# Making the chunk matrices of a delta-rule branch ahead of its value convolutions in a hybrid encoder layer

## The chip, the cores and the metric

The kernel runs on one core of a Trainium2 chip. The metric is the device time of one execution in microseconds (us). The engines are named as in the profile: PE (TensorE, matrix products), DVE (VectorE), ACT (ScalarE), POOL (GpSimd) and SP (SyncE, whose queue issues the transfers). The times of before are a median of three runs and one profiled execution.

## The reference

One layer on 1024 tokens of width 1024, in float32. `h` is the normalised input; one combined projection of `h` feeds three mixers and their gates.

```python
h = rms_norm(x, mix_norm_w)
dn_qkv, dn_z, dn_b, dn_a, a_q, a_k, a_v, x_q, gate_logits = split(h @ w_in)
# A: bidirectional gated delta rule, 4 heads of 128, chunks of 64 tokens
dq, dk, dv = split(silu(centred_depthwise_conv(dn_qkv, w)))      # 5 taps
dq, dk = l2_normalize(dq), l2_normalize(dk)
lmat = where(strict, (kb @ kc.T) * decay, 0)      # 64 x 64 for each chunk, head and direction
sol = triangular_solve(lmat, [vb, kb * exp(gc)])  # unit lower triangular
attn_intra = (qc @ kc.T) * decay                  # then a scan over the 16 chunks, both ways
# B: attention, 8 query and 2 key heads of 64: rms_norm of q and k, axial rotation, softmax
# C: cross attention, 4 heads of 128, into 256 memory tokens
merged = sum(gates * (branches @ w_branch)); x = x + merged @ w_out
x = x + square(relu(rms_norm(x) @ w_up)) @ w_down
out = rms_norm(x, final_norm_w)
```

## The kernel before

Every product is made of three: each operand is split into a high and a low part (`split`: ACT casts the high part, DVE or POOL subtracts for the low part), and `gemm` sums high·high, low·high and high·low in PSUM. Weights arrive as `w_raw` (512 KB) by `wunit` or `wtok`.

The order of each engine's instructions is fixed when the kernel is built: a scheduler follows the dependencies and its own estimate of times, and within an engine instructions run in that order, one after the other. All transfers are issued on SP's queue.

The stages before the scan, with the names that the prediction uses:

- **Start** (L229 to L285). Eight tiles `xt` of 128 tokens are loaded, squared and summed on ACT (`jk`), scaled by their norm factor and by the norm weight `wbc` on DVE (L278), and transposed by PE into `hTh` and `hTl`.
- **Convolutions.** `conv_tile(ct)` projects 128 channels with 48 matmuls of 512 columns, and forms five taps on DVE: L404 multiplies the first, L409 adds the four others; L417 and L418 finish. Tiles 0 to 7 are queries and keys, 8 to 11 the values; the latter go to `vn_d` in memory.
- **Preparation.** `prep(m)`, once for each of eight pairs of chunks: products of keys and queries (`kq`) and a sum of log decays (`rb`, made by POOL) on PE, `df` and `dd` on DVE (L482 to L493), an exponential on ACT, a factor `nbeta` on POOL. The result goes to `at_d` and `xs_d` in memory.
- **Inverse.** `X`, 128 partitions of 64 x 64, is loaded from `xs_d`; each partition holds one matrix. For j from 1 to 62, L705 makes an outer product into `tm` and L706 adds it to `X`; L708 scales `X` by `bcol`, and it goes to `ts_d`. All of it runs on DVE.
- **Beside the inverse** stand generators that are advanced in turn: `keys()` and `queries()` (24 calls of `rope_norm`, whose results `khl` and `qhl` PE transposes), and `gate_z()` (`z_th`), `mem_norm()`, `memory()` (`mTl`, `mhi`, `mlo`) and `queries_x()` (`xh`, `xl`). `rope_norm` copies the projection to `r_x` (ACT), multiplies it by two rows of the rope table (POOL, L560 and L561), squares and sums each head (ACT, L563), adds the parts (DVE, L568 and L569) and multiplies by the factor of each head (DVE, L570).
- **Gates.** `gates()` makes the matmuls of the three gates; `fill(n)` takes some of them where PE would have none. Then follow the scan (which reads `ts_d`), the two attentions, the branch products, the output projection and the feed-forward part. At the end each of eight tiles `o` is scaled by its norm factor and stored (`finish`, L1148).

Of the kernel before, what the change touches and what calls it, by code (L numbers as in the profile page):

```python
# [9 lines left out]
F32 = mybir.dt.float32  # L10
F32R = mybir.dt.float32r
# [75 lines left out]
def hybrid_block(tc, x, mem, mix_norm_w, w_in, dn_conv_w, dn_a_log, dn_dt_bias, dn_norm_w, q_norm_w, k_norm_w,  # L87
# [147 lines left out]
    wdn = cor.tile([P, 1], F32, name="wdn")  # L235
    ld(out=wdn, in_=dn_norm_w.rearrange("o d -> d o"))
    dve.tensor_scalar(out=wdn, in0=wdn, scalar1=0.5, scalar2=None, op0=ALU.mult)

    tst = ExitStack()
    tkp = pool(tst, "tkp", bufs=2)  # L240

    def wtok(c0):
        hi = tkp.tile([P, 8, 256], F32R, name="t_hi", tag="t_hi", bufs=1)
        lo = tkp.tile([P, 8, 256], F32R, name="t_lo", tag="t_lo", bufs=1)
        for k in range(0, 8, 4):
            raw = wst.tile([P, 4, 256], F32, name="w_raw", tag="w_raw")
            ld(out=raw, in_=w_in[k * P:(k + 4) * P, c0:c0 + 256].rearrange("(k p) c -> p k c", p=P))
            split(hi[:, k:k + 4], lo[:, k:k + 4], raw, wlo[0])
        return hi, lo

# [3 lines left out]
    p0 = pool(st, "p0", bufs=2, side="right")  # L254
    first = {}
    wbc = p0.tile([P, D], F32, name="wbc", bufs=1)
    for m in range(8):
        if m == 0:
            xts = []
            for i in range(8):  # L260
                xt = p0.tile([P, D], F32, name="xt", tag="xt", bufs=8)
                ld_rows(xt, x, i)
                xts.append(xt)
                if i == 0:
                    ld(out=wbc, in_=mix_norm_w.broadcast_to([P, D]))
                if i == 1:
                    braw = wst.tile([P, 8, 64], F32, name="w_raw", tag="w_raw")
                    bhl = tkp.tile([P, 8, 128], F32R, name="b_hl", tag="t_hi", bufs=1)
                    ld(out=braw, in_=w_in[:, C_BA:C_BA + 64].rearrange("(k p) c -> p k c", p=P))
                    split(bhl[:, :, 0:64], bhl[:, :, 64:128], braw)  # L270
                if i == 3:
                    wlo[0] = gp
                    for ct in (4, 0):
                        first[ct] = wunit(w_in[:, ct * P:(ct + 1) * P], 8, P)
                    wlo[0] = None
# [117 lines left out]
    def conv_tile(ct):  # L393
# [70 lines left out]
    def prep(m):  # L464
# [87 lines left out]
    def rope_norm(hi, lo, src, nh, tab, m, sc, bi):  # L552
# [139 lines left out]

    sst = ExitStack()
    sv = pool(sst, "sv", side="right")
    X = sv.tile([P, 64, 64], F32, name="X")
    tm = sv.tile([P, 1024], F32, name="tm")
    bcol = sv.tile([P, 64], F32, name="bcol")
    ld(out=X, in_=xs_d.rearrange("m f a r c -> (m f a) r c"))
    for m in range(8):
        for f in range(2):  # L700
            ld(out=bcol[m * 16 + f * 8:m * 16 + f * 8 + 8], in_=bt_d[:, m, :, f])
    for j in range(1, 63):
# [439 lines left out]
    def factor(m, j):  # L1142
# [96 lines left out]
```

## Time and profile before

| | us |
|---|---|
| median of 3 runs | 1975.61 (1975.19 to 1977.64) |
| the profiled execution | 1976.33 |
| its span, first to last instruction | 1974.5 |
| PE busy | 1900.6 (96%) |
| DVE busy | 1169.2 (59%) |
| ACT busy | 731.8 (37%) |
| POOL busy | 397.2 (20%) |

The difference between span and time of the execution, 1.8 us, is what lies around the first and the last instruction. The granted TensorE clock is 0.988 of full speed in the mean. Busy time is an average over stages; the rows further below take single stages out of it.

### The profile page before, as it was taken

To read this page: it belongs to the slowest core of one execution; us is meant where nothing else is said; L and a number is where in the kernel's file an instruction comes from. 1 tells how busy PE (TensorE), PEld (TensorE's weight loads), DVE (VectorE), ACT (ScalarE), POOL (GpSimd) and SP (SyncE) were. 2 spreads that over 40 slices of the span, in tenths; PEclk is the share of its full clock that TensorE was granted. 3 is DMA by queue.
4 is the path that set the end of the run, shared out by engine and by line. 5 is a ranking of instruction groups with operands and counts; after the bars stand their busy time and mean duration, and the time that the engine had idled before them with its cause. 6 is when DMAs were issued, how large, how long until landed. Compare 5 with 4: busy or idle time off the path is not lost.

```text
span 1974.5 us, 26282 instructions
## 1 busy us (share of the span) xinstructions
PE 1900.6 (96%) x10229; PEld 1611.6 (82%) x10229; DVE 1169.2 (59%) x1701; ACT 731.8 (37%) x1453; POOL 397.2 (20%) x309
## 2 busy tenths in 40 slices
PE   6999897799999999999999999999999999999997
PEld 5888787688998888888888878888888888888885
DVE  4778879993576666666635463444443444444445
ACT  4344343332555666666642131321121212112124
POOL 3003657851251000000000520100010101001013
PEclk9999998899999999999999999999999999999998
DMA  8235743447654222222146455231111102121113
GB/s 170 76 107 149 226 139 110 118 127 243 191 163 133 85 94 75 86 75 86 59 150 201 157 180 161 74 120 40 55 54 33 54 33 65 43 64 46 41 43 86
DMA packets 232893, 207.82 MB, mean 105 GB/s; under 512 B 44800, under 2 KB 196544, under 8 KB 232256
## 3 DMA queue, kind: packets, MB, share of 16 engines
q1 hardware_dynamic: 232768, 206.13, 34.7%
q8 instruction: 81, 1.33, 0.3%
q14 instruction: 44, 0.36, 0.1%
HBM read 148.91 MB, written 57.18 MB: 104 GB/s over the span
## 4 chain that ended last, share of the span: by engine, by line
PE 74%; DVE 6%; POOL 3%; DMA 2%; issue 2%; ACT 1%; SPq 0%; POOLq 0%; DVEq 0%; ACTq 0%
PE ps L81 40%; PE ps_mm L81 20%; PE ps_t L84 3%; PE ps_sm L81 3%; PE ps_t L81 3%; PE ps_s L81 3%; PE ps_sp L81 2%; DVE tm L705 2%; DVE X L706 1%; POOL r_t L560 1%; DMA w_raw<-in_w_out_dram 1%; POOL r_t L561 1%; POOL r_rs L138 0%; DMA X<-xs_d 0%; DVE o L1152 0%
## 5 line engine op out<-in xcount | busy, mean ns | idle before, releaser
L81 PE MATMUL ps_mm<-hTh,w_hi 128*128 128x512 f32 x704 | 286.1, 406 | 3.5 <-ACT hTh L141 3.4
L81 PE MATMUL ps_mm<-hTl,w_hi 128*128 128x512 f32 x704 | 283.9, 404 | 0.0
L81 PE MATMUL ps_mm<-hTh,w_lo 128*128 128x512 f32 x704 | 277.7, 395 | 2.4 <-POOL w_lo L142 2.4
L1140 DVE TENSOR_TENSOR o<-o,ps 128x512 f32<-128x512 f32 (+1 forms) x257 | 171.3, 683 | 97.0 <-PE ps L81 95.5
L81 PE MATMUL ps<-hfh,w_hi 128*128 128x512 f32 x512 | 199.6, 391 | 0.0
L81 PE MATMUL ps<-wdh,al 128*128 128x512 f32 (+1 forms) x514 | 199.6, 389 | 0.0
L81 PE MATMUL ps<-wdl,ah 128*128 128x512 f32 (+1 forms) x514 | 199.6, 389 | 0.0
L81 PE MATMUL ps<-hfl,w_hi 128*128 128x512 f32 x512 | 199.6, 390 | 0.0
L81 PE MATMUL ps<-hfh,w_lo 128*128 128x512 f32 x512 | 199.5, 390 | 0.0
L142 POOL TENSOR_TENSOR wdl<-w_raw,wdh 128x1024 fp32r<-128x1024 f32 x32 | 76.4, 2397 | 601.1 <-ACT wdh L141 601.1
L81 PE MATMUL ps<-wdh,ah 128*128 128x512 f32 (+1 forms) x514 | 188.7, 389 | 0.0
L1132 ACT ACTIVATE f_r<-ps 128x512 f32<-128x512 f32 x64 | 38.1, 595 | 363.7 <-PE ps L81 363.7
L142 DVE TENSOR_TENSOR w_lo<-w_raw,w_hi 128x1024 fp32r<-128x1024 f32 x78 | 100.0, 1282 | 121.0 <-ACT w_hi L141 120.6
L141 ACT CAST w_hi<-w_raw 128x1024 fp32r<-128x1024 f32 x96 | 100.9, 1051 | 171.6 <-PE ps_mm L81 104.0
L1133 DVE TENSOR_TENSOR f_r<-f_r 128x512 f32<-128x512 f32 x64 | 55.3, 865 | 183.3 <-ACT f_r L1132 183.3
L81 PEld LDWEIGHTS ps_mm<-hTh,w_lo 128*128 128x128 f32 x704 | 133.7, 190 | 28.0 <-POOL w_lo L142 2.6
L81 PEld LDWEIGHTS ps_mm<-hTh,w_hi 128*128 128x128 f32 x704 | 133.7, 190 | 27.9 <-ACT hTh L141 3.8
L81 PEld LDWEIGHTS ps_mm<-hTl,w_hi 128*128 128x128 f32 x704 | 133.9, 190 | 20.2
L1072 POOL TENSOR_TENSOR g_acc<-g_acc,g_l 128x512 f32<-128x512 f32 x28 | 41.4, 1481 | 509.8 <-ACT g_yh L141 475.4
L142 DVE TENSOR_TENSOR ptl<-ps_t,pth 128x512 fp32r<-128x512 f32 x128 | 86.6, 687 | 60.0 <-ACT pth L141 59.7
L81 PEld LDWEIGHTS ps<-wdh,al 128*128 128x128 f32 x514 | 96.6, 188 | 19.9
L81 PEld LDWEIGHTS ps<-wdh,ah 128*128 128x128 f32 x514 | 96.5, 188 | 19.8
(288 smaller groups left out, 4045.9 us busy)
## 6 DMA issues: line engine op xcount, KB each, us to landing
w_raw<-in_w_in_dram SPq DMA_DIRECT2D x50, 512.0 KB, 4.1
w_raw<-in_w_up_dram SPq DMA_DIRECT2D x32, 512.0 KB, 4.1
w_raw<-in_w_down_dram SPq DMA_DIRECT2D x32, 512.0 KB, 3.6
g_d<-gt SPq DMA_DIRECT2D x48, 256.0 KB, 2.0
g_l<-g_d SPq DMA_DIRECT2D x24, 512.0 KB, 3.4
w_raw<-in_w_branch_dram SPq DMA_DIRECT2D x12, 512.0 KB, 4.1
y_raw<-y_d SPq DMA_DIRECT2D x12, 512.0 KB, 3.6
xt<-in_x_dram SPq DMA_DIRECT2D x16, 256.0 KB, 9.9
```

Of the source, the lines that this page charges most:

```text
L81: return self._put(self.tc.nc.tensor.matmul(*a, **k))
L84: return self._put(self.tc.nc.tensor.transpose(*a, **k))
L141: act.copy(out=hi, in_=src)
L142: (eng or dve).tensor_tensor(out=lo, in0=src, in1=hi.bitcast(F32), op=ALU.subtract)
L560: gp.tensor_tensor(out=t1, in0=x0, in1=bc(tab[:, 0, m], 1, nh), op=ALU.mult)
L561: gp.tensor_tensor(out=t2, in0=x0, in1=bc(tab[:, 1, m], 1, nh), op=ALU.mult)
L705: dve.tensor_tensor(out=t, in0=bc(X[:, j + 1:, j], 2, j), in1=bc(X[:, j, 0:j], 1, n), op=ALU.mult)
L706: dve.tensor_tensor(out=X[:, j + 1:, 0:j], in0=X[:, j + 1:, 0:j], in1=t, op=ALU.add)
L1072: (dve if bi == 2 and mt > 5 else gp).tensor_tensor(out=acc[mt][:, c], in0=acc[mt][:, c], in1=t, op=ALU.add)
L1132: act.activation(out=r, in_=ps, func=AF.Relu)
L1133: dve.tensor_tensor(out=r, in0=r, in1=r, op=ALU.mult)
L1140: dve.tensor_tensor(out=o[m][:, c], in0=o[m][:, c], in1=ps, op=ALU.add)
```

## The change

Five pieces:

1. Start: all `xt` tiles are allocated first; the norm weight comes as one row of 4 KB, which PE multiplies by a column of ones into 128 partitions (two matmuls, two copies on ACT), where 512 KB were loaded before. Transfers are issued in another order. The first halves of two convolution projections are made straight behind the transposes (`head`).
2. The first tap of a convolution is an ACT instruction (12 in all).
3. `prep` for all eight pairs, and the load of `X` and `bcol`, stand ahead of the value convolutions. `X`, `tm` and `bcol` therefore have memory of their own from early on, and the pool `tkp` (rope table, weights of keys and queries) is opened only when the pools of the convolutions are closed.
4. L570 becomes one ACT instruction for each head (four for a query unit, two for a key unit).
5. The end: the last two tiles are finished behind the loop, tile 7 first; the first half of each is stored by ACT's queue, the second by SP's.

```diff
+    sst = ExitStack()
+    sv = pool(sst, "sv")
...
+    ld_rows(xts[0], x, 0)
+    ld(out=wrow, in_=mix_norm_w)
+    ld(out=ca, in_=ca_d)
...
+        pe.matmul(ps, lhsT=one1, rhs=wrow[:, c:c + 512], start=True, stop=True)
+        act.copy(out=wbc[:, c:c + 512], in_=ps)
...
-                    ld(out=wbc, in_=mix_norm_w.broadcast_to([P, D]))
...
+    head = {}
+    for ct in (4, 0):
+        head[ct] = ps_mm()
+        proj_ch(head[ct], *first[ct], 0)
...
-        dve.tensor_scalar(out=acc, in0=xn, scalar1=cw[:, ct, 2:3], scalar2=None, op0=ALU.mult)
+        act.activation(out=acc, in_=xn, func=AF.Copy, scale=cw[:, ct, 2:3])
...
+    for m in range(8):
+        prep(m)
+
+    X = sv.tile([P, 64, 64], F32, name="X")
...
+    ld(out=X, in_=xs_d.rearrange("m f a r c -> (m f a) r c"))
...
     for h in range(4):
         vt = to_token(conv_tile(8 + h))
         ld(out=dram_tiles(vn_d, h), in_=tiles(vt))
-    for m in range(8):
-        prep(m)
 
     cst.close()
     prs.close()
     gst.close()
+    tst = ExitStack()
+    tkp = pool(tst, "tkp", bufs=2, side="right")
...
-        dve.tensor_tensor(out=x0, in0=x0, in1=bc(rs, 2, 64), op=ALU.mult)
+        for h in range(nh):
+            act.activation(out=x0[:, h], in_=x0[:, h], func=AF.Copy, scale=rs[:, h:h + 1])
...
+    def store(q, m, c):
+        for h, j in enumerate((m, 15 - m)):
+            q.dma_start(out=out[j * 64:(j + 1) * 64, c], in_=o[m][h * 64:(h + 1) * 64, c])
...
+        if m > 5:
+            store(act, m, slice(0, 512))
...
+            store(nc.sync, m, slice(512, 1024))
```

Three places show how the order of the instructions moves. PE at the first preparation, before: `ps_mm` is a convolution's projection (here the last of them), `kq` the first product of a preparation, `rb` the sum of decays; `ps_mm_2087` is a projection of the z gate.

```order
L81 MATMUL ps_mm_1611<-hTh1_150,w_lo_1577 128x512
L81 MATMUL ps_mm_1611<-hTh1_150,w_hi_1576 128x512
L81 MATMUL ps_mm_1611<-hTl1_152,w_hi_1576 128x512
L81 MATMUL ps_mm_1611<-hTh1_150,w_lo_1577 128x512
L81 MATMUL ps_dn_1663<-kq_1660 64x64 x9
L84 MATMUL ps_t_1562<-ca_73,c_x_1496 128x128 x4
L84 MATMUL ps_t_1568<-ca_73,c_x_1496 128x128 x4
L81 MATMUL ps_dn_1663<-kq_1660 64x64 x7
L81 MATMUL ps_dn_1680<-rb_1681,onb_394 128x512
L81 MATMUL ps_dn_1680<-rb_1684,onb_394 128x512
L81 MATMUL ps_dn_1703<-kq_1700 64x64 x16
L81 MATMUL ps_mm_2087<-hTh0_149,w_hi_2082 128x512
```

The same place on PE with the change; `ps_mm_1848` is the third value convolution.

```order
L81 MATMUL ps_mm_1848<-hTh0_147,w_hi_1840 128x512
L81 MATMUL ps_mm_1848<-hTl0_149,w_hi_1840 128x512
L81 MATMUL ps_mm_1848<-hTh0_147,w_lo_1841 128x512
L81 MATMUL ps_mm_1848<-hTh0_147,w_hi_1840 128x512
L84 MATMUL ps_t_1741<-ca_73,c_x_1675 128x128 x2
L81 MATMUL ps_dn_1332<-kq_1329 64x64 x16
L81 MATMUL ps_dn_1349<-rb_1350,onb_453 128x512
L81 MATMUL ps_dn_1349<-rb_1353,onb_453 128x512
L81 MATMUL ps_dn_1372<-kq_1369 64x64 x16
L84 MATMUL ps_t_1741<-ca_73,c_x_1675 128x128 x2
L84 MATMUL ps_t_1747<-ca_73,c_x_1675 128x128 x4
L81 MATMUL ps_mm_1848<-hTl0_149,w_hi_1840 128x512
```

Before, all 576 convolution matmuls stand ahead of the first `kq`; now 493 do, and 84 follow between the preparations.

SP around the load of `X`, before: `at_d` and `xs_d` are results of preparations, `ka_d`, `kb_d` and `vz_d` those of key units, `bcol` a factor of the inverse.

```order
L97 DMA vz_d_124<-vt_2150 128x128
L97 DMA at_d7_117<-dd_1968 128x512
L97 DMA vz_d_124<-vt_2235 128x128
L97 DMA vz_d_124<-vt_2326 128x128
L97 DMA xs_d_118<-dd_1968 64x8x64 x2
L97 DMA ka_d_122<-kab_2121 256x1x128
L97 DMA kb_d_123<-kab_2121 256x1x128
L97 DMA vz_d_124<-vt_2411 128x128
L97 DMA X_4243<-xs_d_118 128x4096
```

With the change: `mt` are the memory tokens, `mwb` their norm weight, `w_raw` the first two weights of the z gate.

```order
L97 DMA at_d7_115<-dd_1637 128x512
L97 DMA xs_d_116<-dd_1637 64x8x64 x2
L97 DMA X_1649<-xs_d_116 128x4096
L97 DMA vn_d_106<-c_tok_1995 128x8x128
L97 DMA mwb_2020<-in_mem_norm_w_dram 128x1024
L97 DMA mt_2022<-in_mem_dram 128x1024
L97 DMA mt_2035<-in_mem_dram 128x1024
L97 DMA rope_2048<-in_rope_dram 128x1024
L97 DMA qkw_2051<-in_q_norm_w_dram 128x64
L97 DMA qkw_2051<-in_k_norm_w_dram 128x64
L97 DMA w_raw_2114<-in_w_in_dram 128x8x128
L97 DMA w_raw_2292<-in_w_in_dram 128x8x128
```

The loads of memory tokens, rope table and z weights, which stood far ahead of the `X` load, now stand behind it.

DVE at the end of the inverse, before: L708 is the last instruction on `X`; `xl` is the low part of a cross-attention query, `w_lo` that of a weight of the gates, `u` (L787) belongs to the scan.

```order
L705 TENSOR_TENSOR tm_4244<-X_4243 128x236
L142 TENSOR_TENSOR xl_4233<-ps_mm_4207,xh_4232 128x512
L706 TENSOR_TENSOR X_4243<-X_4243,tm_4244 128x4x59
L705 TENSOR_TENSOR tm_4244<-X_4243 128x180
L706 TENSOR_TENSOR X_4243<-X_4243,tm_4244 128x3x60
L705 TENSOR_TENSOR tm_4244<-X_4243 128x122
L706 TENSOR_TENSOR X_4243<-X_4243,tm_4244 128x2x61
L705 TENSOR_TENSOR tm_4244<-X_4243 128x62
L706 TENSOR_TENSOR X_4243<-X_4243,tm_4244 128x62
L708 TENSOR_TENSOR X_4243<-X_4243,bcol_4245 128x4096
L142 TENSOR_TENSOR w_lo_5922<-w_raw_5920,w_hi_5921 128x1024
L142 TENSOR_TENSOR w_lo_5984<-w_raw_5982,w_hi_5983 128x1024
```

With the change (L720, L721 and L723 are the former L705, L706 and L708; L591, L592 and L597 the former L568, L569 and L573):

```order
L720 TENSOR_TENSOR tm_1650<-X_1649 128x62
L721 TENSOR_TENSOR X_1649<-X_1649,tm_1650 128x62
L591 TENSOR_TENSOR r_x_3639<-r_t1_3640,r_t2_3641 128x8x16
L592 TENSOR_TENSOR r_x_3639<-r_t1_3640,r_t2_3641 128x8x16
L723 TENSOR_TENSOR X_1649<-X_1649,bcol_1651 128x4096
L597 TENSOR_TENSOR qhl_3539<-r_x_3540,qhl_3539 128x4x64
L140 TENSOR_TENSOR xl_3793<-ps_mm_3767,xh_3792 128x512
L597 TENSOR_TENSOR qhl_3638<-r_x_3639,qhl_3638 128x4x64
L591 TENSOR_TENSOR r_x_3738<-r_t1_3739,r_t2_3740 128x8x16
L592 TENSOR_TENSOR r_x_3738<-r_t1_3739,r_t2_3740 128x8x16
L140 TENSOR_TENSOR xl_3881<-ps_mm_3855,xh_3880 128x512
L591 TENSOR_TENSOR r_x_3832<-r_t1_3833,r_t2_3834 128x8x16
```

Before, eight `xl` and 16 `qhl` stand ahead of the last `X` instruction; now eight `qhl` and no `xl`.

## Rows read from the trace of the kernel before

**Rows 1.** The page: busy us, share of the span and instructions by engine.

```profile
PE 1900.6 (96%) x10229; PEld 1611.6 (82%) x10229; DVE 1169.2 (59%) x1701; ACT 731.8 (37%) x1453; POOL 397.2 (20%) x309
```

**Rows 2.** Windows: length, busy us (count) of PE, PEld, DVE, ACT, POOL; clock, DMA.

```profile
195.00:252.00 57.00, 51.40 (x428) 43.07 (x428) 51.20 (x66) 19.56 (x40) 37.96 (x36) 0.97 0.71 210
...
268.00:459.00 191.00, 160.67 (x1015) 145.27 (x1014) 184.96 (x225) 71.08 (x243) 124.72 (x93) 0.93 0.42 124
459.00:475.00 16.00, 16.00 (x77) 13.04 (x76) 2.90 (x2) 3.77 (x6) 1.49 (x2) 1.00 0.94 308
500.00:550.00 50.00, 50.00 (x463) 47.61 (x463) 29.07 (x77) 25.65 (x78) 15.47 (x15) 1.00 0.67 195
```

**Rows 3.** Waits of PE from 195 to 460 us: total, times, longest.

```profile
PE ps_t L84 <- DVE qhl L573: 20.5, 7, 7.6
PE ps_dn L84 <- DVE mTl L142: 6.4, 1, 6.4
```

**Rows 4.** The chain that ended last, at the gates: start, length, what.

```profile
442.28 31.36 PE ps_mm L81 x137
```

**Rows 5.** Timeline of DVE: start, length, instruction, idle before and its releaser.

```profile
195.98 0.68 DVE L482 TENSOR_TENSOR df<-ps_dn,gc 128x512 f32<-128x512 f32 x1
250.98 0.67 DVE L493 TENSOR_TENSOR dd<-ps_dn,dd 128x512 f32<-128x512 f32 x1
267.57 0.26 DVE L705 TENSOR_TENSOR tm<-X 128x62 f32<-128x62 f32 x1 [5.06 <-DMA X<-xs_d]
454.44 4.43 DVE L708 TENSOR_TENSOR X<-X,bcol 128x4096 f32<-128x4096 f32 x1
```

**Rows 6.** Groups of DVE: three from 195 to 460 us, two (L409) from 150 to 195.

```profile
L486 DVE SCALAR_TENSOR_TENSOR dd<-df,ca 128x256 f32<-128x256 f32 x16 | 16.8, 1086 | 0.0
L484 DVE TENSOR_TENSOR dd<-df,ca 128x512 f32<-128x512 f32 x8 | 7.2, 898 | 0.3
...
L482 DVE TENSOR_TENSOR df<-ps_dn,gc 128x512 f32<-128x512 f32 x8 | 5.4, 678 | 0.0
...
L409 DVE SCALAR_TENSOR_TENSOR c_acc<-c_x,cw,c_acc 128x1022 f32<-128x1022 f32 x8 | 10.9, 1367 | 0.2
L409 DVE SCALAR_TENSOR_TENSOR c_acc<-c_x,cw,c_acc 128x1023 f32<-128x1023 f32 x6 | 9.9, 1646 | 0.2
```

**Rows 7.** Groups of DVE from 267.5 to 459 us.

```profile
L706 DVE TENSOR_TENSOR X<-X,tm 128x62 f32<-128x62 f32 (+30 forms) x62 | 68.3, 1102 | 1.1
L705 DVE TENSOR_TENSOR tm<-X 128x62 f32<-128x62 f32 (+30 forms) x62 | 68.0, 1096 | 5.9 <-DMA X<-xs_d 5.1
L570 DVE TENSOR_TENSOR r_x<-r_x,r_rs 128x256 f32<-128x256 f32 (+1 forms) x19 | 17.8, 938 | 1.9 <-POOL r_rs L138 1.8
L573 DVE TENSOR_TENSOR qhl<-r_x,qhl 128x256 fp32r<-128x256 f32 x16 | 10.4, 648 | 0.0
...
L142 DVE TENSOR_TENSOR xl<-ps_mm,xh 128x512 fp32r<-128x512 f32 x8 | 5.5, 682 | 0.0
```

**Rows 8.** A group of POOL from 267.5 to 459 us; L561 is its equal.

```profile
L560 POOL TENSOR_TENSOR r_t<-r_x,ropeq 128x256 f32<-128x256 f32 x16 | 20.8, 1299 | 13.2 <-ACT r_x L559 13.2
```

**Rows 9.** Timelines of DVE and of POOL around 284 us.

```profile
282.38 0.75 DVE L706 TENSOR_TENSOR X<-X,tm 128x572 f32<-128x572 f32 x1
...
284.13 2.87 DVE L706 TENSOR_TENSOR X<-X,tm 128x612 f32<-128x612 f32 x1
287.04 2.91 DVE L705 TENSOR_TENSOR tm<-X 128x650 f32<-128x650 f32 x1
...
283.41 5.85 POOL L142 TENSOR_TENSOR t_lo<-w_raw,t_hi 128x1024 fp32r<-128x1024 f32 x2
```

**Rows 10.** A group of ACT from 195 to 460 us.

```profile
L563 ACT ACTIVATE r_x<-r_x 128x64 f32<-128x64 f32 x80 | 19.6, 248 | 27.3 <-POOL r_t L561 27.0
```

**Rows 11.** Timeline of ACT at the start: the cast of the second weight.

```profile
28.64 1.05 ACT L141 CAST w_hi<-w_raw 128x1024 fp32r<-128x1024 f32 x1 [0.63 <-DMA w_raw<-in_w_in_dram]
```

**Rows 12.** The stores at the end, from 1950 us: duration ns min/median/max, starts.

```profile
L97 SPq DMA_DIRECT2D out_dram<-o x18: 466/570/1568, 1950.0 to 1971.2; - x18
```

More of the change, by code (lines that the diff above doesn't have):

```diff
@@ L120, in hybrid_block @@
     ca = con.tile([P, CA_N], F32, name="ca")
-    ld(out=ca, in_=ca_d)
     ident = ca[:, CA_ID:CA_ID + 128]
@@ L126, in hybrid_block @@
     identr = con.tile([P, P], F32R, name="identr")
-    act.copy(out=identr, in_=ident)
     mhalf = con.tile([P, 64], F32, name="mhalf")
@@ L235, in hybrid_block @@
     wdn = cor.tile([P, 1], F32, name="wdn")
[L236 to L249, printed above, removed]
+    sst = ExitStack()
+    sv = pool(sst, "sv")
     gst = ExitStack()
@@ L255, in hybrid_block @@
     first = {}
+    xts = [p0.tile([P, D], F32, name="xt", tag="xt", bufs=8) for _ in range(8)]
     wbc = p0.tile([P, D], F32, name="wbc", bufs=1)
-    for m in range(8):
[L258 to L264, printed above, removed]
-                    ld(out=wbc, in_=mix_norm_w.broadcast_to([P, D]))
[L266 to L275, printed above, removed]
+    wrow = p0.tile([1, D], F32, name="wrow", bufs=1)
+    one1 = p0.tile([1, P], F32, name="one1", bufs=1)
+    gp.memset(one1, 1.0)
+    ld_rows(xts[0], x, 0)
+    ld(out=wrow, in_=mix_norm_w)
+    ld(out=ca, in_=ca_d)
+    for i in range(1, 4):
+        ld_rows(xts[i], x, i)
+    for c in range(0, D, 512):
+        ps = ps_mm()
+        pe.matmul(ps, lhsT=one1, rhs=wrow[:, c:c + 512], start=True, stop=True)
+        act.copy(out=wbc[:, c:c + 512], in_=ps)
+    act.copy(out=identr, in_=ident)
+    wlo[0] = gp
+    first[4] = wunit(w_in[:, 4 * P:5 * P], 8, P)
+    for i in range(4, 6):
+        ld_rows(xts[i], x, i)
+    first[0] = wunit(w_in[:, 0:P], 8, P)
+    for i in range(6, 8):
+        ld_rows(xts[i], x, i)
+    wlo[0] = None
+    for m in range(8):
         xt = xts[m]
@@ L285, in hybrid_block @@
     st.close()
+    braw = wst.tile([P, 8, 64], F32, name="w_raw", tag="w_raw")
+    bhl = gpl.tile([P, 8, 128], F32R, name="b_hl", bufs=1)
+    ld(out=braw, in_=w_in[:, C_BA:C_BA + 64].rearrange("(k p) c -> p k c", p=P))
+    split(bhl[:, :, 0:64], bhl[:, :, 64:128], braw)
+    ld(out=wdn, in_=dn_norm_w.rearrange("o d -> d o"))
+    dve.tensor_scalar(out=wdn, in0=wdn, scalar1=0.5, scalar2=None, op0=ALU.mult)
     def proj_tok(ps, wh, wl, m):
@@ L398, in conv_tile @@
         for f in range(2):
-            ps = ps_mm()
-            proj_ch(ps, wh, wl, f)
+            ps = head.pop(ct, None) if f == 0 else None
+            if ps is None:
+                ps = ps_mm()
+                proj_ch(ps, wh, wl, f)
             pv = ps.rearrange("p (m h c) -> p m h c", h=2, c=64)
@@ L497, in prep @@
             ld(out=xs_d[m, f].rearrange("a r c -> r a c"), in_=dd[r, 1].rearrange("p y h c -> p (y h) c"))
+    for m in range(8):
+        prep(m)
+    X = sv.tile([P, 64, 64], F32, name="X")
+    tm = sv.tile([P, 1024], F32, name="tm")
+    bcol = sv.tile([P, 64], F32, name="bcol")
+    ld(out=X, in_=xs_d.rearrange("m f a r c -> (m f a) r c"))
+    for m in range(8):
+        for f in range(2):
+            ld(out=bcol[m * 16 + f * 8:m * 16 + f * 8 + 8], in_=bt_d[:, m, :, f])
     for h in range(4):
@@ L509, in hybrid_block, with wtok @@
     gst.close()
+    tst = ExitStack()
+    tkp = pool(tst, "tkp", bufs=2, side="right")
+    def wtok(c0):
+        hi = tkp.tile([P, 8, 256], F32R, name="t_hi", tag="t_hi", bufs=1)
+        lo = tkp.tile([P, 8, 256], F32R, name="t_lo", tag="t_lo", bufs=1)
+        for k in range(0, 8, 4):
+            raw = wst.tile([P, 4, 256], F32, name="w_raw", tag="w_raw")
+            ld(out=raw, in_=w_in[k * P:(k + 4) * P, c0:c0 + 256].rearrange("(k p) c -> p k c", p=P))
+            split(hi[:, k:k + 4], lo[:, k:k + 4], raw, wlo[0])
+        return hi, lo
     wlo[0] = gp
@@ L689, in fill @@
             next(gt, None)
[L693 to L701, printed above, removed]
     for j in range(1, 63):
@@ L1146, in factor @@
         return rs
+    def store(q, m, c):
+        for h, j in enumerate((m, 15 - m)):
+            q.dma_start(out=out[j * 64:(j + 1) * 64, c], in_=o[m][h * 64:(h + 1) * 64, c])
     def finish(m):
-        i = act.activation(out=o[m][:, 0:512], in_=o[m][:, 0:512], func=AF.Copy, scale=rs3[m])
-        if m == 6:
-            tc.keep_in_program_order(i)
+        act.activation(out=o[m][:, 0:512], in_=o[m][:, 0:512], func=AF.Copy, scale=rs3[m])
+        if m > 5:
+            store(act, m, slice(0, 512))
         dve.scalar_tensor_tensor(out=o[m][:, 512:1024], in0=o[m][:, 512:1024], scalar=rs3[m], in1=lwb[:, 512:1024],
                                  op0=ALU.mult, op1=ALU.mult)
-        if m < 6:
+        if m > 5:
+            store(nc.sync, m, slice(512, 1024))
+        else:
             ld_rows(o[m], out, m, store=True)
-        else:
-            for c in (slice(512, 1024), slice(0, 512)):
-                ld_rows(o[m], out, m, c, store=True)
     lwb = None
@@ L1203, in hybrid_block @@
                         gp.tensor_tensor(out=o[m][:, c], in0=o[m][:, c], in1=lwb[:, c], op=ALU.mult)
-            if last:
+            if last and m < 6:
                 rs3[m] = factor(m, len(cs))
-                if m < 6:
-                    finish(m)
+                finish(m)
+    for m in (6, 7):
+        rs3[m] = factor(m, len(cs) - 7 + m)
+    finish(7)
     finish(6)
-    finish(7)
     top.close()
```

## The prediction, made before the changed kernel ran

> **What bounds the kernel now.** I read the page's first part, then the windows, the waits of PE in the stretch where it idles, the chain, and the groups of DVE and POOL there. PE is busy 1900.6 us of the 1974.5 us span [rows 1], so about 74 us is idle. Some 19 us of that lies before the projections start and 14 us behind the last matmul. The rest is nearly all between 195 and 459 us: 57 − 51.40 and 191 − 160.67, some 36 us [rows 2]. There DVE is the bound: 51.20 of 57 us, then 184.96 of 191 us. PE waits for what DVE hands it, 20.5 us for `qhl` and 6.4 us for `mTl` [rows 3]. After 459 us PE is full (16.00 of 16, and 50.00 of 50 in the scan) [rows 2], and the gate matmuls that fill PE from 442.28 us on, 31.36 us for 137 or 0.229 us each [rows 4], are only a filler: what of them is not done before the scan is done in it, at full price.
>
> So the time is that at which the inverse ends (T, 458.87 us: the last `X` instruction, 4.43 us from 454.44 us [rows 5]), plus the PE work that is still to do then. The change must be judged on both: T moves earlier, and work that stood before T may stand behind it.
>
> **The change, part by part.**
>
> *Preparation starts earlier.* The first `df` stands at 195.98 us [rows 5]. In the new order of PE the first chunk products stand in the middle of the third value convolution, with 493 instead of all 576 convolution matmuls ahead of them: 83 × 0.229 = 19 us. DVE has lost the first taps too, so that it lags a little less. I take 175 us; the start of the program is neutral (below).
>
> *Preparation and the rest of the value convolutions.* Now on DVE in one stretch: eight preparations, each 0.68 + 0.90 + 2 × 1.09 for L482 to L486 [rows 6] and 2 × 0.67 for L491 and L493 [rows 5] = 5.1 us, so 41 us; ten taps at 1.37 to 1.65 us, 15 us [rows 6]; three pairs of closing products, some 4 us: 60 us. Both prices hold their part of the contention with POOL (an undisturbed `df` pair of L486 would be 0.87 us, not 2.18 us). With eight preparations at 3.6 us and taps at 1.28 us the sum is 46 us. POOL has less to do there than before (no weight splits of the z gate, no rope), but its own `rb` and `nbeta` products remain. I take 55 us, range 46 to 60. PE has only about 31 us of work in it: the other 84 convolution matmuls (19 us), the preparations' own (9 us), transposes (3 us). In the stretch of before it had z and key units as well. About 25 us of PE idle is new here.
>
> *From the last `dd` to the first step of `X`.* Before: 250.98 + 0.67 = 251.65 to 267.57 us, 15.9 us for the store, the load and their latency [rows 5]. The same path stands in the change; 15 us. On SP, however, the memory tokens, the rope table and the z weights, which had landed by then, stand behind the `X` load, and the rope weights come after it too. For these 15 us PE has hardly anything.
>
> *The inverse.* 191.3 us from 267.57 to 458.87 us; DVE is busy 185 of it, 136.3 us with the `X` steps [rows 7]. By the new order what stands on DVE between the first and the last `X` instruction changes so. Leaving: 19 × L570, 17.8 us; all eight `xl`, 5.5 us; eight of 16 `qhl`, 5.2 us [rows 7]; two weight splits and one `mlo`, 3 us. Coming: five key units' `khl` and five `z_th` at about 0.65 us, 6.4 us; two scalings of the memory tokens, 2.6 us. Net −22.5 us, so 169 us. The POOL work in it stays about equal: six query units with 2 × 1.30 us [rows 8] leave (−16 us), five key units, two rope products and two weight splits come (+17 us). So I leave the contention as it is, and add 3 us for key and z weights that now land late: 172 us.
>
> How far contention can go: undisturbed steps cost 0.26 us for 62 elements and 0.75 us for 572 [rows 5, 9], or 0.2 us + 0.00096 us per element; over 124 steps with 83,328 elements that is 105 us, against 136 us. 31 us is lost to POOL. One place shows how: while POOL made two `t_lo` from 283.41 us for 5.85 us, an `X` step of 612 elements took 2.87 us and its neighbour 2.91 us, some 4.2 us more than undisturbed [rows 9]: 71% of POOL's time. Without any of it the inverse takes 172 − 31 = 141 us.
>
> The Trainium skill ("SBUF — State Buffer", Who interferes with whom) says that a DVE instruction with two inputs from SBUF contends with a GpSimd instruction that reads SBUF, by an exclusive lock on a shared port pair: the later of the two to issue blocks fully until the first is done. The trace agrees in kind and shows 71% instead of all; by the full rule the inverse would take 13 us more (31 / 0.71 = 44 us). The rule speaks against packing two-operand DVE work next to POOL work, as this change does in the preparation.
>
> *T.* 175 + 55 + 15 + 172 = 417 us, 42 us earlier than 458.87 us.
>
> *What is late next.* At T the old kernel had finished all projections of this part and 16.6 us of gates (442.28 to 458.87 us [rows 4]). In the new order of DVE all eight `xl`, and the last six `qhl` that are interleaved with them, stand behind the last `X` instruction, and on PE six projections of 24 matmuls (6 × 24 × 0.229 = 33 us), three query units (72 matmuls of half the width, 8 us) and transposes (3 us) cannot run before them: 44 to 45 us. With the gates that makes 45 + 16.6 = 61 us of PE work that moved behind T. Everything behind T is PE's, so it costs its full length. −42 + 61 = +19 us. With the tail (below) break-even is T = 400 us.
>
> *The scaling by the norm factor on ScalarE* (L570): four `ACTIVATE` per unit instead of one DVE multiplication of 0.94 us mean. The nearest row, the squares of the same 64 columns, is 0.248 us each [rows 10], so 1 us per unit; ACT is busy 71 of 191 us there [rows 2], its cover, and the query chain that PE waits for stays equally long. If that cover failed, it would cost 24 × 0.1 us, nothing that counts. *First taps on ScalarE:* 12 × some 1.1 us (a pass over 1024 elements is 1.05 us [rows 11]); ACT has room. 0 us beyond what the earlier start has.
>
> *Start.* PE runs on without gaps from 30 us, held by `x` and by the casts of the first weights (28.64 us, which waited for its DMA [rows 11]). 4 KB instead of 512 KB for the norm weight frees the queue, but two `w_hi` casts now stand on ACT ahead of `hTh` casts and wait for their transfers. Between −2 and +3 us; I take 0.
>
> *Tail.* The last stores are issued on SP one behind the other, 0.57 us median each [rows 12]; four of eight go to ACT's queue. −2 us, between 0 and −3.
>
> Sum: 1976.33 + 19 − 2 = 1993.3 us for the profiled execution, whose span lacks 1.8 us of it; the median lies 0.7 us lower. **1992.6 us.**
>
> **Rivals.**
>
> *Contention goes away* (faster). Preparation 46 us, inverse 141 us: T = 175 + 46 + 15 + 141 = 377 us, −82 + 61 − 2 = −23 us, 1953 us. For it: POOL has less to do in the preparation. Against: POOL's large instructions in the inverse are as many as before. The middle of it, T at 390 us, gives 1966 us. It decides faster from T below some 396 us. 0.23.
>
> *Break-even.* T between 396 and 404 us, where the two moves cancel: 1972 to 1980 us. 0.08.
>
> *Full exclusion* (slower still). All of POOL's time lost instead of 71%: 31 / 0.71 = 44 us in place of 31 in the inverse, 60 us in the preparation: T = 435 us, 2011 us. For it: the preparation and taps are of the kind that loses. Against: the 71%. 0.11. (The lock as the Trainium skill states it, "SBUF — State Buffer", Who interferes with whom, is this case.)
>
> *The change doesn't bring the inverse forward.* On DVE the steps of `X` stand right behind the last value convolution, with no later work ahead of them; a load of `X` that waits for other transfers is a few us, inside my range. No chance of its own.
>
> **How the numbers follow.** Forecast 0.58, between 1980 and 2004 us (preparation 50 to 60, inverse 163 to 178, start −2 to +3); contention gone 0.23; break-even 0.08; full exclusion 0.11. A measurement here can tell about 0.2% (4 us) from no change. Faster 0.23, same 0.08, slower 0.69. The range leaves out the better part of either end: 1957 to 2010 us.
>
> **What would show it.** First `df` near 175 us, first `X` step near 245 us, `X` scaled by 417 us; PE with 20 us or more idle on both sides of the `X` load; `xl` behind the last `X` row, and gates not started before T + 40 us. Steps of `X` with a total near 105 instead of 136 us would prove the forecast wrong, as would PE full around the `X` load, or PE waiting in the scan, which would make the moved work free.

## The result, and the profile after

The changed kernel takes 2010.35 us (median of 4 runs, 2009.53 to 2012.10) against 1976.62 us of before beside it: a ratio of 1.0171 (95% interval 1.0154 to 1.0189), 34 us slower. The forecast had the direction and the mechanism, and half the size: 1992.6 us, +17 us, with 2010 us as the end of the range.

The page of the changed kernel, its first part (busy us, share, instructions; it answers to [rows 1]):

```profile
span 2007.7 us, 26328 instructions
...
PE 1910.9 (95%) x10233; PEld 1614.0 (80%) x10233; DVE 1159.3 (58%) x1665; ACT 766.7 (38%) x1547; POOL 401.2 (20%) x310
```

The span grew by 33.2 us. 10.3 us of it is PE busy longer with the same matmuls but four, and 22.9 us is PE idle more (96.8 in place of 73.9 us). Where, and at what clock, the windows of the changed kernel tell (columns as in [rows 2]):

```profile
195.00:228.00 33.00, 14.46 (x138) 10.80 (x136) 31.77 (x39) 10.29 (x14) 16.36 (x11) 0.76 0.39 119
228.00:240.50 12.50, 1.94 (x8) 1.57 (x8) 1.29 (x2) 1.67 (x3) 0.25 (x1) 0.50 0.74 227
240.50:262.00 21.50, 16.69 (x107) 15.78 (x108) 20.83 (x20) 8.22 (x18) 18.52 (x12) 0.79 0.49 163
262.00:432.50 170.50, 144.16 (x904) 130.74 (x904) 164.61 (x180) 75.10 (x262) 116.34 (x90) 0.91 0.38 107
```

From 195 to 240.5 us PE is busy 16.4 of 45.5 us: first DVE has preparation and taps to do, then the `X` matrices are on their way. The granted clock falls to 0.50 there, the lower of the two levels, 1.2 of 2.4 GHz, and stands at 0.91 in the rest of the inverse (0.93 before, [rows 2]).

The waits of PE from 150 to 420 us, the longest four (answers to [rows 3]):

```profile
PE ps_t L84 <- DVE c_x L422: 18.7, 2, 15.7
PE ps_t L84 <- DVE qhl L597: 11.9, 6, 3.8
PE ps_dn L81 <- ACT t_hi L139: 11.6, 2, 11.2
PE ps_t L84 <- DVE khl L599: 10.2, 3, 5.8
```

The first is the wait for the last value convolution behind the preparations on DVE. The third is the key weight: its cast on ACT starts at 242.02 us, held by the store of the last value tile, whose memory the opened pool uses again, and that store was issued behind the `X` load:

```profile
242.02 1.99 ACT L139 CAST t_hi<-w_raw 128x1024 fp32r<-128x1024 f32 x2 [9.49 <-DMA vn_d<-c_tok]
```

DVE's timeline of the changed kernel at the four points of the forecast (answers to [rows 5]):

```profile
171.78 0.68 DVE L486 TENSOR_TENSOR df<-ps_dn,gc 128x512 f32<-128x512 f32 x1
...
225.48 0.68 DVE L497 TENSOR_TENSOR dd<-ps_dn,dd 128x512 f32<-128x512 f32 x1
...
240.58 0.26 DVE L720 TENSOR_TENSOR tm<-X 128x62 f32<-128x62 f32 x1 [10.76 <-DMA X<-xs_d]
...
427.96 4.42 DVE L723 TENSOR_TENSOR X<-X,bcol 128x4096 f32<-128x4096 f32 x1
```

| stage | forecast, us | measured, us |
|---|---|---|
| first `df` | 175 | 171.8 |
| preparation and value convolutions | 55 | 54.4 |
| last `dd` to first step of `X` | 15 | 14.4 |
| the inverse | 172 | 191.8 |
| its end T | 417 | 432.4 |
| from T to the end, against before | +59 | +59.7 |

The last row is the time of the profiled execution less T: 2009.53 − 432.38 = 1577.15 us, and 1976.33 − 458.87 = 1517.46 us before. So one term failed. The inverse was to lose 19 us and lost nothing (191.3 us before). The groups of DVE in it, changed kernel (answers to [rows 7]; L720 and L721 are the former L705 and L706, L591 and L597 the former L568 and L573):

```profile
L721 DVE TENSOR_TENSOR X<-X,tm 128x62 f32<-128x62 f32 (+30 forms) x62 | 73.9, 1192 | 1.2
L720 DVE TENSOR_TENSOR tm<-X 128x62 f32<-128x62 f32 (+30 forms) x62 | 70.1, 1130 | 12.1 <-DMA X<-xs_d 10.8
L591 DVE TENSOR_TENSOR r_x<-r_t,r_t 128x128 f32<-128x128 f32 (+1 forms) x18 | 11.9, 663 | 1.9 <-ACT r_x L586 1.9
...
L597 DVE TENSOR_TENSOR qhl<-r_x,qhl 128x256 fp32r<-128x256 f32 x9 | 6.6, 734 | 0.0
L649 DVE SCALAR_TENSOR_TENSOR z_th<-z_th,ps_mm 128x512 f32<-128x512 f32 x8 | 5.4, 680 | 0.1
L551 DVE SCALAR_TENSOR_TENSOR mt<-mt,rs,mwb 128x1024 f32<-128x1024 f32 x2 | 4.9, 2451 | 0.0
```

The multiplications by the norm factor are gone (17.8 us), and the steps of `X` are 7.7 us longer than before (144.0 in place of 136.3), L591 takes 0.66 us where L568 took 0.33, and so on. What reads one operand from PSUM (`z_th`) costs 0.68 us as ever.

### The profile page after: what moved, and what is told of

Same layout as the page of the kernel before. It is cut to its first block, busy times and chain, and to the rows that moved or that the text cites. A ratio compares the mean times of both kernels' runs of the same rounds, so it can differ in the third digit from the quotient of the medians.

```text
span 2007.7 us, 26328 instructions
## 1 busy us (share of the span) xinstructions
PE 1910.9 (95%) x10233; PEld 1614.0 (80%) x10233; DVE 1159.3 (58%) x1665; ACT 766.7 (38%) x1547; POOL 401.2 (20%) x310
## 5 line engine op out<-in xcount | busy, mean ns | idle before, releaser
L81 PEld LDWEIGHTS ps<-wdl,ah 128*128 128x128 f32 x514 | 96.5, 188 | 19.9
```

What stands on the lines that cost most here:

```text
L81: return self._put(self.tc.nc.tensor.matmul(*a, **k))
```

## The experiments

Two theories of the inverse were to be told apart. **A**: an instruction owns its contended time; move it off DVE, and all of it is gained. **B**: DVE loses a fixed share of POOL's large instructions, whichever of its own happens to stand there; move an instruction, and only its undisturbed time is gained. The share, from the groups of before: the steps of `X` lose 31 us; L570 would cost 16 × 0.41 + 3 × 0.28 = 7.4 us undisturbed (its shortest instances) and loses 10.4; `qhl` loses 3.8 and the rest 1; some 46 us against 89 us of POOL's `w_lo` (33.3), `t_lo` (12.4) and rope products (20.8, 20.5, 1.5 and 0.9), 0.5 us for each. A third question was which piece of the change makes the loss, and whether PE's hole around the `X` load is the loss itself. Each kernel had runs of before beside it.

**Which piece.** `early` is the kernel before with piece 3 alone:

```diff
+    for m in range(8):
+        prep(m)
+    X = sv.tile([P, 64, 64], F32, name="X")
...
+    ld(out=X, in_=xs_d.rearrange("m f a r c -> (m f a) r c"))
     for h in range(4):
         vt = to_token(conv_tile(8 + h))
         ld(out=dram_tiles(vn_d, h), in_=tiles(vt))
-    for m in range(8):
-        prep(m)
...
-    tst = ExitStack()
-    tkp = pool(tst, "tkp", bufs=2)
```

> The kernel before with piece 3 alone (preparation and the load of X ahead of the value convolutions, the rope pool opened late). If piece 3 makes the loss: the work behind T (about 60 us) is the same as in the changed kernel, T comes later by the first taps on DVE (some 4 us) and by the multiplications (6 us by theory B, 17 us by theory A), the tail gives 2 us back: 2022 us (B) or 2033 us (A). If piece 3 is harmless: 1976 us.

Measured: 2013.29 us, ratio 1.0193 (1.0162 to 1.0223), which is nearest to the first case and 9 us below its lower figure. The inverse started 1.5 us earlier than in the changed kernel (239.06 us) and took 194.1 us, 2.3 us more with the multiplications back on DVE, so that T came 0.8 us later (433.14 us) and not some 10; from T to the end it took 1581.0 us, 3.9 us more. `late` is the changed kernel with the same lines moved back.

> The changed kernel with piece 3 undone, all else kept (start, taps and scaling on ACT, tail). If piece 3 makes the loss: before less the tail (1 to 2 us), less what the inverse gains by the multiplications that left DVE: 7 us by theory B, so 1967 us; 18 us by theory A, so 1957 us. If the loss is in the other pieces: about 2010 us.

Measured: 1975.06 us, ratio 0.9992 (0.9977 to 1.0007). Piece 3 makes the whole loss (+36 us alone), and the four others together win nothing that can be told. In `late` the inverse takes 186.3 us, 5 us less than before and not the 18 us of theory A; the forecast of B for the time (1967 us) was too good, since the inverse started 4.4 us later there (272.0 us; from the first `df` to the last `dd` it took 60.7 us against 55.7 before).

**What moving the scaling is worth.** `bact` is the kernel before with piece 4 alone:

```diff
-        dve.tensor_tensor(out=x0, in0=x0, in1=bc(rs, 2, 64), op=ALU.mult)
+        for h in range(nh):
+            act.activation(out=x0[:, h], in_=x0[:, h], func=AF.Copy, scale=rs[:, h:h + 1])
```

> The kernel before with piece 4 alone: the scaling of the rope units on ACT. Theory A (contended price, 17.8 us saved): inverse 173 us, time 1959 us. Theory B (undisturbed price, 16 x 0.41 + 3 x 0.28 = 7.4 us saved, the X steps take over the contention): inverse 184 us, X steps longer than 136 us, time 1970 us.

Measured: 1974.16 us, ratio 0.9993 (0.9981 to 1.0004). Its DVE timeline and its groups in the inverse:

```profile
263.42 0.27 DVE L706 TENSOR_TENSOR tm<-X 128x62 f32<-128x62 f32 x1 [3.48 <-DMA bcol<-bt_d]
...
445.66 4.42 DVE L709 TENSOR_TENSOR X<-X,bcol 128x4096 f32<-128x4096 f32 x1
```

```profile
L707 DVE TENSOR_TENSOR X<-X,tm 128x62 f32<-128x62 f32 (+30 forms) x62 | 75.4, 1216 | 1.2
L706 DVE TENSOR_TENSOR tm<-X 128x62 f32<-128x62 f32 (+30 forms) x62 | 68.6, 1106 | 4.8 <-DMA bcol<-bt_d 3.5
L574 DVE TENSOR_TENSOR qhl<-r_x,qhl 128x256 fp32r<-128x256 f32 x16 | 12.2, 768 | 0.9 <-ACT qhl L572 0.8
```

The inverse is 186.7 us. 17.8 us of work left DVE and 4.6 us were gained: the steps of `X` took over 7.7 us (144.0 in place of 136.3 [rows 7]) and `qhl` 1.8 us. That is B, and a little below it. The time did not follow, though, against the 1970 us of B: the inverse also started 4.1 us earlier, T came 8.8 us earlier (450.08 us), and from T to the end it took 1523.3 us, 5.8 us more than before. Most of what T gained was PE work that no longer fitted ahead of it.

`kdve` is the reverse, the changed kernel with the multiplication back on DVE.

> The changed kernel with piece 4 undone: the scaling of the rope units by the norm factor is one DVE multiplication again (24 in all). Theory A, each instruction owns its contended time: the inverse, 191.8 us in the changed kernel, gets 18 x 0.94 = 17 us longer, and the time follows, 2027 us. Theory B, DVE loses a fixed share of POOL's large instructions whichever of its own stands there: only the undisturbed time of the multiplications comes back (10 x 0.41 + 8 x 0.28 = 6.3 us), the inverse is about 198 us, the time 2017 us, and the steps of X get cheaper by some 8 us. If the inverse doesn't set the time: 2010 us.

Measured: 2017.22 us, ratio 1.0210 (1.0181 to 1.0238). The inverse took 198.8 us, 7.0 more than in the changed kernel, where 15.7 us of multiplications came back:

```profile
L720 DVE TENSOR_TENSOR X<-X,tm 128x62 f32<-128x62 f32 (+30 forms) x62 | 74.3, 1199 | 1.1
L719 DVE TENSOR_TENSOR tm<-X 128x62 f32<-128x62 f32 (+30 forms) x62 | 64.1, 1033 | 11.9 <-DMA X<-xs_d 10.8
L593 DVE TENSOR_TENSOR r_x<-r_x,r_rs 128x256 f32<-128x256 f32 (+1 forms) x19 | 15.7, 827 | 1.2 <-POOL r_rs L136 1.2
```

The steps of `X` fell from 144.0 to 138.4 us beside them. The expectation of B held in the inverse and the time; the steps fell by 5.6 us where some 8 were expected.

**What POOL's work is worth.** `dsplit` (changed kernel), `bdsplit` (kernel before) and `ldsplit` (`late`) make the low parts of the weights beside the inverse on DVE, so that the fuller engine gets more:

```diff
-    wlo[0] = gp
+    wlo[0] = None
 
     mst = ExitStack()
```

> The changed kernel with the weight splits beside the inverse (14 w_lo and 6 t_lo, 54.9 us of POOL) made by DVE, 20 x 1.22 = 24 us more for the engine that is already full there. Theory A: the inverse is 24 us longer, 216 us, time 2034 us. Theory B (0.55 us of DVE lost per us of large POOL work): 24 - 0.55 x 54.9 = -6 us, inverse 186 us, time 2004 us, with the X steps at some 120 us in place of 144.

> The kernel before with nothing changed but the engine of the weight splits beside keys, queries, memory and cross-attention queries: DVE in place of POOL. Theory B: POOL loses some 46 us of large work, DVE gains 25 us less than it loses in contention, PE's idle 36 us between 195 and 459 us shrinks to some 15 us: 1957 us. Theory A: DVE is the bound there, +20 us: 1997 us.

> The run late (preparation where it was) with the weight splits beside the inverse on DVE. PE idles 21 us between 300 and 450 us in late. Theory B (contention follows POOL's large work): most of it goes, 1957 us. Theory A (DVE is full, 18 splits are 22 us more): 1997 us.

Measured: `dsplit` 1981.30 us, 1.0025 (1.0011 to 1.0039); `bdsplit` 1961.92 us, 0.9937 (0.9923 to 0.9952); `ldsplit` 1960.20 us, 0.9920 (0.9903 to 0.9937). A is refuted three times. DVE in the inverse of `dsplit`:

```profile
L721 DVE TENSOR_TENSOR X<-X,tm 128x62 f32<-128x62 f32 (+30 forms) x62 | 61.4, 990 | 0.9
L720 DVE TENSOR_TENSOR tm<-X 128x62 f32<-128x62 f32 (+30 forms) x62 | 55.8, 900 | 11.9 <-DMA X<-xs_d 10.8
L140 DVE TENSOR_TENSOR w_lo<-w_raw,w_hi 128x1024 fp32r<-128x1024 f32 x16 | 20.7, 1296 | 1.6 <-ACT w_hi L139 1.6
```

The steps of `X` take 117.2 us in place of 144.0, where 105 us would be undisturbed. The inverse itself is as long as in the changed kernel (192.6 us), but it holds 22 splits, six more query units and four `xl`. So less is left behind T: 1550 us from T to the end in place of 1577. B was right on the steps and wrong on the rest: it forecast 2004 us because it counted what DVE saves, not the PE work that then fits ahead of T. PE's windows, `dsplit` first, then the changed kernel:

```profile
250.00:300.00 50.00, 48.50 (x280) 42.29 (x279) 48.30 (x63) 19.83 (x68) 24.72 (x27) 1.00 0.37 104
300.00:350.00 50.00, 48.26 (x362) 45.46 (x361) 46.02 (x58) 28.76 (x98) 25.79 (x26) 1.00 0.41 120
```

```profile
250.00:300.00 50.00, 42.47 (x231) 36.18 (x230) 46.47 (x50) 16.59 (x54) 35.76 (x30) 0.93 0.30 83
300.00:350.00 50.00, 42.58 (x256) 37.91 (x255) 48.47 (x49) 18.64 (x56) 30.06 (x21) 0.90 0.36 106
```

`ldsplit` and `bdsplit` beat both kernels; the second is one word away from the kernel before. In `bdsplit` T came only 3.5 us earlier (455.39 us), but PE was busy 420.2 us ahead of it in place of 403.2: the gain is PE work that fits ahead of T. How much of that is owed to DVE losing less, and how much to weights that are ready sooner (a split takes 1.3 us on DVE and 2.8 on POOL), no run separates.

**Which DVE instructions lose.** `pstm` puts `tm` into PSUM, so that the addition of a step reads one operand from SBUF and one from PSUM; this needs PSUM, and `psctl`, with the same fewer buffers and `tm` in SBUF, is its control.

```diff
-        return pp.tile([P, 512], F32, name="ps_dn", tag="dn", bufs=4)
+        return pp.tile([P, 512], F32, name="ps_dn", tag="dn", bufs=3)
...
-        return pp.tile([P, 512], dt, name="ps_t", tag="tt")
+        return pp.tile([P, 512], dt, name="ps_t", tag="tt", bufs=1)
...
-    tm = sv.tile([P, 1024], F32, name="tm")
+    tm = pp.tile([P, 1024], F32, name="tm", bufs=1)
```

> Control for the next run: the changed kernel with fewer PSUM buffers for the small products (three in place of four, and one in place of two for transposes), tm still in SBUF. Both theories: inverse as in the changed kernel, 192 us; 2010 us or a few us more.

> As the control, with tm (the outer product of each step of the inverse) in PSUM, so that the second instruction of a step has one operand in SBUF and one in PSUM in place of two in SBUF. If two operands from SBUF are what lets POOL hold DVE up: the 62 additions fall from 73.9 us to about 53 us and the outer products stay near 70 us; inverse 20 us shorter than the control's, time 20 us less, 1990 us. If any DVE work loses to POOL alike: both groups stay, time as the control. If PSUM costs DVE more by itself: the additions get longer than 53 us undisturbed, and nothing is won.

Measured: `psctl` 2120.28 us, 1.0727 (1.0711 to 1.0743); `pstm` 2109.14 us, 1.0668 (1.0650 to 1.0686). The control costs 110 us, far more than the few us expected: with one buffer for transposes PE waits all through the kernel (52.9 us for `ptl` alone). The inverse can still be compared, 191.7 us in `psctl` and 173.2 us in `pstm`; the time fell by 11 us between the two, and not by 20. The additions of all 62 steps, `psctl` first (shortest, median and longest, ns):

```profile
L721 DVE TENSOR_TENSOR X<-X,tm x62: 276/1054/3383, 256.1 to 441.7; 128x62 f32<-128x62 f32 x2, 128x122 f32<-128x122 f32 x2, 128x180 f32<-128x180 f32 x2, 128x236 f32<-128x236 f32 x2
```

```profile
L721 DVE TENSOR_TENSOR X<-X,tm x62: 221/932/1189, 254.9 to 422.6; 128x62 f32<-128x62 f32 x2, 128x122 f32<-128x122 f32 x2, 128x180 f32<-128x180 f32 x2, 128x236 f32<-128x236 f32 x2
```

Their sum falls from 77.7 to 52.8 us, the undisturbed price, and the longest from 3.38 to 1.19 us. The outer products, which still read two operands from SBUF, get worse (72.1 to 80.9 us): they take over a part. So the additions lose when both operands come from SBUF, and the loss is only partly conserved when fewer such instructions are there. The Trainium skill ("SBUF — State Buffer", Who interferes with whom) says that a DVE instruction with two inputs from SBUF contends with a GpSimd instruction that reads SBUF, and that one with at most one such input does not, outside the modes of DVE that use two ports; the trace agrees for the additions (77.7 and 52.8 us). Two tensors from SBUF are no condition for every DVE instruction: the first tap of the kernel before, which reads one, takes 0.74 us at its shortest and took 2.45 us beside a `w_lo`, which POOL had begun at 179.38 us and ended at 181.77 us. In which mode it ran no trace shows.

```profile
179.87 2.45 DVE L404 TENSOR_SCALAR c_acc<-c_x,cw 128x1024 f32<-128x1024 f32 x1 [0.49 <-ACT c_x L403]
```

**Is the hole the loss?** `hole` is the changed kernel with three units of gate weights (144 matmuls) emitted between the value convolutions and the key units; `hdsplit` is that with the splits on DVE.

```diff
+    gt = gates()
...
+    fill(144)
+
     cst.close()
     prs.close()
     gst.close()
     tst = ExitStack()
```

> The changed kernel with the first 144 gate matmuls emitted between the value convolutions and the key units, where PE is idle for 33 of 50 us (200 to 250 us) around the load of X. If that hole is what the change costs, the gates (33 us) come out of the PE work behind the inverse: 1978 us. If the hole only moves on (weights of z gate and keys queue behind those of the gates): 2000 us or more.

> The run hole with the weight splits beside the inverse made by DVE as well. The two causes lie in different stretches (200 to 250 us; 250 to 450 us), so their gains should add: 1981 - 31 = 1950 us. If DVE, now full with splits, is held up by the extra weights of the gates: 1965 to 1980 us.

Measured: `hole` 2015.20 us, 1.0199 (1.0184 to 1.0215); `hdsplit` 1988.44 us, 1.0070 (1.0055 to 1.0085), worse than `dsplit`. `hole` came out by its second case (2000 us or more), `hdsplit` by neither of its two. The hole was filled all the same, as windows of `hole` show:

```profile
200.00:250.00 50.00, 42.80 (x241) 34.57 (x241) 36.39 (x47) 17.03 (x23) 17.59 (x11) 0.96 0.65 208
350.00:400.00 50.00, 35.31 (x223) 32.36 (x222) 49.18 (x53) 24.10 (x97) 34.00 (x26) 0.86 0.31 94
450.00:500.00 50.00, 44.89 (x254) 37.42 (x253) 10.55 (x21) 24.97 (x84) 23.11 (x27) 0.97 0.68 204
1000.00:1100.00 100.00, 90.25 (x475) 74.28 (x475) 59.48 (x85) 49.86 (x82) 0.00 (x0) 0.95 0.35 120
```

PE is busy 42.80 us from 200 to 250 us, against 17.07 us in the changed kernel. But 5 us each are lost again from 350 to 400 and from 450 to 500 us, and 10 us from 1000 to 1100 us, where the changed kernel had 40.72, 50.00 and 99.96 us: the gates are filler wherever they stand, and what is spent early is missing later. The counts of the two traces bear that out: ahead of T `hole` starts 2303 matmuls and the changed kernel 2212, 91 more and not 144, and behind T PE is idle 34.2 us in place of 18.1. What holds PE up there was not tried by itself. From T (434.65 us) to the end it takes 1581 us, 4 us more than in the changed kernel, though 33 us of gates were done. So filling PE around the `X` load pays nothing by itself.

## Why the prediction was right or wrong

**Direction and mechanism: right.** T came earlier by 26.5 us, 59.7 us moved behind it; −26.5 + 59.7 = +33.2 us, which is the difference of the two profiled executions. That the time is T plus the PE work behind it held, and the size of that work too (61 us less 2 us in the forecast). Behind T all is PE's, as foretold: it is busy 70.00 of 70 us from 430 to 500 us. The first gate is evaluated at 484.7 us, T + 52 us (the forecast: not before T + 40 us).

**Start, preparation, `X` load: right** within some 3 us each. PE is idle 18.5 us from 195 to 228 us and 10.6 us up to the first step; the forecast had 25 and nearly 15 us. (An undisturbed pair of L486 is 0.95 us, two at the shortest 0.474 us of the trace of before, and not 0.87; the 3.6 us for a preparation holds with it.)

**The inverse: wrong, and it is the whole miss.** The step that failed is the pair "Leaving: 19 × L570, 17.8 us" and "So I leave the contention as it is". 17.8 us is a contended price; 10.4 us of it was POOL's, and stays on DVE with whatever stands there next. `bact` measures the piece alone: 4.6 us, so 13 us of the 19.8 us miss. The other 7 us fit POOL's side of that step, which was to be equal (+1 us) and is not. POOL in the inverse of the changed kernel:

```profile
L140 POOL TENSOR_TENSOR w_lo<-w_raw,w_hi 128x1024 fp32r<-128x1024 f32 x14 | 38.7, 2767 | 13.1 <-ACT w_hi L139 13.1
...
L140 POOL TENSOR_TENSOR t_lo<-w_raw,t_hi 128x1024 fp32r<-128x1024 f32 x6 | 16.2, 2727 | 14.9 <-ACT t_hi L139 14.9
L584 POOL TENSOR_TENSOR r_t<-r_x,ropeq 128x256 f32<-128x256 f32 x10 | 13.0, 1295 | 0.0
...
L583 POOL TENSOR_TENSOR r_t<-r_x,rope 128x128 f32<-128x128 f32 x8 | 9.2, 1156 | 22.8 <-ACT r_x L582 22.8
```

With the two groups like these, 11.8 and 8.3 us, and the two products of the rope table, 5.4 us, that makes 102.6 us against some 89 us before: four weight splits were added (`w_lo` from 12 to 14, `t_lo` from four to six) where the forecast counts two, and a key unit's products cost 2.2 us together where 1.5 us had been read off one place. 13 us at 0.5 is 7 us. No run takes this added work out alone, but the loss can be counted in the traces. Price each DVE instruction between the first and the last `X` instruction at the shortest one of its operands and shape in any of the traces, and call the rest of its time lost; price POOL's weight splits and rope products likewise (us):

| kernel | DVE, undisturbed | DVE, lost | POOL's splits and rope products, undisturbed | lost for each |
|---|---|---|---|---|
| before | 149.9 | 48.2 | 62.1 | 0.78 |
| `bact` | 142.5 | 47.2 | 62.1 | 0.76 |
| `late` | 141.7 | 47.7 | 62.1 | 0.77 |
| changed | 137.8 | 56.9 | 72.9 | 0.78 |
| `kdve` | 146.1 | 60.1 | 75.8 | 0.79 |
| `early` | 145.8 | 58.1 | 74.4 | 0.78 |

(Recorded times of neighbours overlap by a few hundredths of a us, so these sums lie 9 to 13 us above DVE's busy time.) Whatever leaves or joins DVE, the loss goes with POOL's work. The forecast, with 10.4 of the 48.2 us leaving with L570 and nothing coming, implied some 38 us; the changed kernel loses 56.9. These 19 us are the miss: 10.4 that stayed, and 8.7 that came with 10.8 us more of POOL's work (13 and 7 by the length of the inverse in `bact`).

**The reading of 71%: wrong.** The prediction took the trace to show that DVE loses 71% of POOL's time and not all. One weight split shows what happens, two timelines of the kernel before:

```profile
361.58 1.18 DVE L705 TENSOR_TENSOR tm<-X 128x990 f32<-128x990 f32 x1
362.79 3.27 DVE L706 TENSOR_TENSOR X<-X,tm 128x990 f32<-128x990 f32 x1
```

```profile
362.23 2.79 POOL L142 TENSOR_TENSOR w_lo<-w_raw,w_hi 128x1024 fp32r<-128x1024 f32 x1 [1.52 <-ACT w_hi L141]
```

The split takes 2.33 us at its shortest; here it begins while L705 runs, until 362.76 us, and ends 2.26 us after that. L706 then ends 1.04 us after the split (365.02 us), as if it had begun only there (1.18 us, less 0.14). So it is everywhere in the inverse: of the 44 DVE instructions of before that took over 0.2 us more than their shortest, each ends its shortest time, less 0.12 to 0.13 us, after a split or rope product of POOL; so do all 43 of the changed kernel, less 0.11 to 0.19 us. None ends so behind POOL's small instructions (`r_rs`, 128x4, 1.42 us in the mean). The two exclude each other in full, and the recorded 5.85 us of [rows 9] hold POOL's own waiting: undisturbed the two `t_lo` are 4.7 us, of which DVE lost 4.2. A share like B's is what such a stream adds up to, and no constant: in `dsplit`, `ldsplit` and `bdsplit`, where POOL has only the rope products, it is 0.55 to 0.66.

**The rivals.** Full exclusion had the mechanism, as the rows above show, and 2011 us is close to what came, but its sum is right by luck: it wanted 44 us lost in the steps of `X` (31 us divided by 71% of a time that holds POOL's own waits), 60 us of preparation and an inverse of 185 us. Measured are 144.0 − 105 = 39 us, 54.4 us and 191.8 us, and it too let the loss of L570 leave with it. "Contention goes away" is refuted for this change, and `dsplit` shows what it takes. The clock has no term in the forecast. PE is busy 10.3 us longer over the kernel, and ahead of T a mean of 0.92 of the clock was granted, against 0.96 before; but DVE sets the pace there, and the term behind T, where 1.00 was granted, came out as foretold, so no run shows that the clock is part of the miss.

**The small terms.** The tail won 0.6 us, not 2 (from the last matmul's end to the end of the span 14.1 us before, 13.5 us now). ACT issues the stores itself, and its scaling of the last half tile waited 2.77 us behind them (2002.79 us). The start brought seven matmuls more until 50 us (145 against 138, 1.6 us at 0.229 us); in `late` the first `df` stands at 195.59 us, 0.4 us earlier than before, and the time is that of before.

## What to carry to other kernels

Price an instruction that leaves a contended engine at its shortest instance, not at its mean: the difference belongs to the engine that disturbs, and stays. If the bound engine stands still while a neighbour's instruction runs, work that the neighbour does slowly can be better made on the bound engine: in `bdsplit` 18 splits added 23.6 us to DVE in the inverse, and what it lost fell by 31.8 us (48.2 to 16.4). And a chain that starts earlier wins only what its start brings forward less the work that no longer fits ahead of its end: write down both before moving it.

## What the runs showed of the hardware

- A DVE instruction that reads two operands from SBUF and a large POOL instruction ran one after the other and not side by side: all 44 stretched DVE instructions in the inverse of before end their shortest time, less 0.12 to 0.13 us, after a POOL instruction. Additions of the inverse took up to 3.38 us (1.18 us undisturbed); with one operand in PSUM the same additions took at most 1.19 us, and `z_th`, which reads one from PSUM, took 0.67 to 0.69 us in every run.
- What DVE lost was 0.76 to 0.79 us for each undisturbed microsecond of POOL's splits and rope products in six kernels, and 0.55 to 0.66 in the three kernels without splits on POOL in the inverse.
- One DVE instruction with a single tensor operand from SBUF (L404) was stretched too, from 0.74 to 2.45 us.
- The granted clock fell to its lower level (0.50 from 228 to 240.5 us) where PE had only 1.94 us of work in 12.5 us, and stood at 0.79 in the 21.5 us after that. The same matmuls cost PE 10 us more over the kernel.
